# Gated unit and rotary queries finished in PSUM, rotary cache keys laid out by their loads, attention operands laid anew: one hybrid decoder step

## Chip, cores and metric

The kernel runs on one core of a Trainium2 chip. The metric is the device time of one execution in microseconds (us); the median of three runs stands for the kernel. TensorE (PE) multiplies and transposes into PSUM, VectorE (DVE), ScalarE (ACT) and GpSimd (POOL) work element by element, SyncE (SP) issues most DMAs; ACT and POOL issue some. Each engine runs its own list of instructions in a fixed order and waits on semaphores.

## What is computed

One step of a layer with two branches (an S5 state space and latent attention, MLA) for a prompt of 1024 tokens and for 8 sequences of 8 new tokens with 32 cache pages of 128 tokens each; width 1024, 16 heads, float32. Cut to what matters:

```python
xn = rmsnorm(x, norm_in)
u_s, g_s, cq, ckv_raw, kr_raw, g_a, m_s, m_a = split_in(xn @ w_in)
# S5 branch, then its gated unit
y = S5(u_s);  zg = gelu(y)
y_s = zg * sigmoid(zg @ ssm_w_glu + ssm_b_glu)
y_s = (y_s * silu(g_s)) @ w_br_ssm
# latent attention with rotary parts
cq = rmsnorm(cq, mla_q_norm);  q = einsum('blr,rhd->blhd', cq, mla_w_uq)
q_rope = apply_rope(q[..., QK_NOPE:], cos, sin)
ckv = rmsnorm(ckv_raw, mla_kv_norm);  k_rope = apply_rope(kr_raw, cos, sin)
o = attend(...)   # prompt: causal; new tokens: cached pages (cache_ckv, cache_krope by page_table) and themselves
y_a = (o * silu(g_a)) @ w_br_attn
h = x + (sigmoid(m_s) * y_s + sigmoid(m_a) * y_a) @ w_out;  y = rmsnorm(h, norm_final)
```

Besides `y` the step returns `ckv`, `k_rope` and the last S5 state, for the prompt and for the new tokens.

## The kernel before

A float32 product is made of three passes on float32r operands: each operand is split into a high and a low part (`split`, L96 the cast on ACT, L102 the subtraction on DVE or POOL), and `mm3` (L159) adds high by high, high by low and low by high in one PSUM bank. A weight stripe of 128 columns comes as `wraw`, is split into `whi` and `wlo`, and meets the transposed input `xT` in three chunks of 368, 368 and 352 tokens, 24 matmuls each. There are two PSUM banks of the name `mm` and six more of `tr`, `sc` and `acc`.

The stages are Python generators. `woven` interleaves two of them by weights, a scheduler turns the program into one order per engine, and `pin` holds a PE instruction to its place in the order in which it was written. In the order of time:

- up to 345 us: norm and transposes of x (`stage_x`), the S5 branch, gate stripes; `s5_states` (L780, L785) copies the last states to `sto`, one buffer, and SP writes them to `ssm_sample` and `ssm_prompt`;
- 345 to 480: two gate stripes, then `stage_latents`. `load_wide` (L137) loads the weights of the latents in pieces of 128 columns, `wraw` to `wwhi` and `wwlo`. The page numbers of the cache (`cache_rows`, `sel`, `j16`, `pt`, L1209 to L1219) are computed just ahead. `cqn` is the normed latent (L853, L868; its norm is a power on POOL, L200), transposed on PE at L835. Alongside runs `cache_ropes`: POOL gathers rotary keys of a page block into `dkr` (L1229, two buffers), copies them to `dks` in another order (L1234), PE transposes them (L1239), ACT and DVE split them, and SP writes three parts to `kr_dram` (L1244);
- 480 to 520: `q_rope`, rotary queries in 12 groups. DVE multiplies by the cosine table into `qr` (L904), POOL multiplies the rotated copy `qrot` by the sine table (L903), DVE adds (L905), then ACT and DVE split into `qh` and `ql`. One gate stripe is woven in, a second one is pinned behind;
- 520 to 700: latent queries, keys and values, gate stripes, then `attn_setup` (keys, queries, the `causal` mask at L983) and `dec_setup`, which also makes the rotary keys of the new tokens (`kss`, L1131 to L1136);
- 700 to 1130: the prompt attention (`prompt`: 32 units of head and half), woven with dense stages: gate stripes, the gelu of S5, then from 945 the gated unit `stage_glu`. A list of goals (`PLAN`) says at which mark of the attention each dense group is due;
- 1130 to 1545: `decode` over the 32 page blocks, woven with the end of the gated unit and with both branch products. POOL gathers `ck` (two buffers, L1201); ACT casts it to `ch`, POOL subtracts to `cl`, two halves of 1024 columns per page block (L102); `dec_keys` loads `krT` (L1251);
- to 1758: branch product of the attention and the output.

A gate stripe ends with a pass of ACT (L803) and one of DVE (`gst<-gst,mm`, L804), which empties the `mm` bank. In the gated unit a group ends with L1432 to L1440: ACT writes tanh of the bank to `th`, POOL adds `zz = zh + zl` (L1436), DVE computes `gl = (th + 1) * gl` (L1438) and `zz = zz * gl` (L1439), and SP writes `a_dram`. `gl` holds the gate, loaded from `g_gs` in four buffers.

## Time and profile before

| quantity | value |
|---|---|
| median of 3 runs | 1761.27 us (1760.45 to 1765.47) |
| the profiled execution | 1759.65 us |
| its span, first to last instruction | 1757.8 us |
| mean granted clock of PE | 0.987 |
| PE busy | 1688.1 us, 96% |
| DVE, ACT, POOL busy | 1158.4 (66%), 934.4 (53%), 592.5 us (34%) |
| DMA | 299.52 MB, 258309 packets, mean 170 GB/s |

Busy time counts an engine's instructions without overlap. A granted clock of 1.0 is 2.4 GHz on PE; 0.5 is 1.2 GHz, and a mean between the two is a mix of stretches at either level. In a timeline row the first number is the start in us of the span, the second the duration, and the bracket the idle time of the engine just before, with what ended it.

### The profile page before, as it was taken

How to read it: one execution, taken by the hardware profiler on the slowest of the kernel's cores; microseconds unless marked ns; L12 is line 12 of the kernel's file. 1: busy time of each engine (PE TensorE's matmuls, PEld its weight loads, DVE VectorE, ACT ScalarE, POOL GpSimd, SP SyncE). 2: the span in 40 equal slices, each digit the busy share in tenths (PEclk: the TensorE clock that was granted, in tenths of full speed). 3: DMA queues.
4: the chain of work that ended last, by engine and by line, in shares of the span. 5: the costliest groups of instructions: out<-in, count | busy, mean ns of one | idle time of the engine just before them, and what ended most of it. 6: DMA issues, size and time to landing. Idle time of an engine off the chain costs nothing.

```text
span 1757.8 us, 31271 instructions
## 1 busy us (share of the span) xinstructions
PE 1688.1 (96%) x10954; PEld 1588.1 (90%) x10954; DVE 1158.4 (66%) x2640; ACT 934.4 (53%) x2226; POOL 592.5 (34%) x622
## 2 busy tenths in 40 slices
PE   6999999989999999999998999999999999999997
PEld 5999999989989998999997898998988999899976
DVE  6768898333374343878888788567656666654496
ACT  5146657722354443767777556456656566631144
POOL 1000000013442204656663555654545445400012
PEclk9999999999999999999999999999999999999999
DMA  8555344544478988665667552575555455384322
GB/s 218 123 144 153 110 120 122 144 139 113 138 222 292 315 299 242 159 167 149 189 162 220 141 158 64 179 251 187 179 172 175 156 170 188 120 303 145 101 85 102
DMA packets 258309, 299.52 MB, mean 170 GB/s; under 512 B 40448, under 2 KB 215272, under 8 KB 251880
## 3 DMA queue, kind: packets, MB, share of 16 engines
q1 hardware_dynamic: 247976, 240.90, 47.7%
q0 software_dynamic: 7872, 48.24, 8.1%
q10 hardware_dynamic: 2304, 8.39, 1.3%
q8 instruction: 87, 1.43, 0.4%
q14 instruction: 70, 0.57, 0.1%
HBM read 201.79 MB, written 95.66 MB: 169 GB/s over the span
## 4 chain that ended last, share of the span: by engine, by line
PE 78%; DMA 8%; DVE 4%; issue 4%; ACT 3%; POOL 2%; SPq 1%; POOLq 0%; ACTq 0%; DVEq 0%
PE mm L159 40%; PE sc L1028 5%; PE sc L159 5%; PE acc L1193 4%; PE tr L1064 3%; PE tr L159 3%; DMA ck<-cache_ckv,pidx 2%; PE acc L1077 2%; PE acc L1078 2%; PE sc L1167 2%; PE sc L1256 1%; PE tr L1256 1%; PE tr L1167 1%; POOL cl L102 1%; DMA wraw<-w_in 1%
## 5 line engine op out<-in xcount | busy, mean ns | idle before, releaser
L159 PE MATMUL mm<-xT,whi 128*128 128x368 f32 (+1 forms) x1920 | 503.9, 336 | 8.7 <-ACT xT L253 4.8
L159 PEld LDWEIGHTS mm<-xT,whi 128*128 128x128 f32 x1920 | 340.9, 190 | 12.6 <-ACT xT L253 5.3
L159 PE MATMUL mm<-xT,wlo 128*128 128x368 f32 (+1 forms) x960 | 320.6, 334 | 0.2 <-DVE wlo L102 0.2
L102 POOL TENSOR_TENSOR cl<-ck,ch 128x1024 fp32r<-128x1024 f32 x64 | 154.2, 2411 | 163.8 <-ACT ch L96 149.4
L159 PEld LDWEIGHTS mm<-xT,wlo 128*128 128x128 f32 x960 | 182.4, 190 | 1.6 <-DVE wlo L102 0.5
L96 ACT CAST pTh<-tr 128x256 fp32r<-128x256 f32 (+1 forms) x248 | 110.8, 449 | 85.9 <-PE tr L1064 67.1
L102 DVE TENSOR_TENSOR pTl<-tr,pTh 128x256 fp32r<-128x256 f32 (+1 forms) x248 | 126.3, 512 | 41.2 <-ACT pTh L96 24.2
L1028 PE MATMUL sc<-K,Q 128*128 128x384 f32 (+5 forms) x576 | 131.5, 345 | 4.0 <-ACT p L1040 4.0
L1045 POOL TENSOR_SCALAR p<-p,sm 128x128 f32<-128x128 f32 (+7 forms) x128 | 96.8, 761 | 109.4 <-DVE sm L1044 48.5
L1040 ACT ACTIVATE p<-sc,sm 128x128 f32<-128x128 f32 (+2 forms) x192 | 110.7, 584 | 22.9 <-DVE sm L1035 12.7
L96 ACT CAST whi<-wraw 128x1024 fp32r<-128x1024 f32 (+1 forms) x76 | 73.3, 966 | 93.1 <-PE mm L159 79.9
L1229 POOL DMA_INDIRECT dkr<-cache_krope,pidx x32 | 33.0, 1032 | 264.2 <-DMA gkv<-mla_kv_norm 256.7
L1064 PE MATMUL tr<-ident,p 128*128 128x128 f32 x576 | 112.1, 274 | 7.6 <-DVE pTl L102 6.7
L159 PE MATMUL mm<-z,whi 128*128 128x368 f32 (+1 forms) x384 | 110.4, 349 | 2.3 <-ACT gst L801 2.3
L1032 DVE TENSOR_REDUCE sm<-sc 128x1 f32<-128x128 f32 (+2 forms) x192 | 104.2, 551 | 9.9 <-PE sc L1028 6.8
L159 PE MATMUL mm<-aT,whi 128*128 128x368 f32 (+1 forms) x384 | 107.6, 337 | 1.6 <-ACT th L1432 1.6
L1028 PEld LDWEIGHTS sc<-K,Q 128*128 128x128 f32 x576 | 98.3, 189 | 11.2 <-ACT p L1040 6.3
L159 PE MATMUL mm<-oT,whi 128*128 128x368 f32 (+1 forms) x384 | 94.2, 327 | 0.2 <-DVE gl L1464 0.2
L102 DVE TENSOR_TENSOR wlo<-wraw,whi 128x1024 fp32r<-128x1024 f32 (+1 forms) x54 | 61.6, 1142 | 39.7 <-ACT whi L96 36.1
L1064 PEld LDWEIGHTS tr<-ident,p 128*128 128x128 f32 x576 | 72.2, 140 | 14.3 <-DVE pTl L102 5.1
L96 ACT CAST ch<-ck 128x1024 fp32r<-128x1024 f32 x64 | 67.3, 1053 | 29.1 <-DMA ck<-cache_ckv,pidx 12.7
L1078 PE MATMUL acc<-pTl,Vt 128*128 128x256 f32 (+1 forms) x224 | 81.6, 364 | 0.1
(534 smaller groups left out, 4390.0 us busy)
## 6 DMA issues: line engine op xcount, KB each, us to landing
wraw<-w_in SPq DMA_DIRECT2D x45, 512.0 KB
krT<-kr_dram SPq DMA_DIRECT2D x64, 192.0 KB
kr_dram<-krx SPq DMA_DIRECT2D x64, 128.0 KB
...
```

What stands on the lines that cost most here:

```text
L96: nc.scalar.copy(hi, src)
L102: return e.tensor_sub(lo, src, hi.bitcast(F32))
L159: i = nc.tensor.matmul(ps, row(s, k)[:, wsl], row(m, k)[(slice(None),) + xsl], start=start and k == j == 0, stop=stop and k == nk - 1 and ...
L1028: self.mark(nc.tensor.matmul(s[:, :w], qq[:, i * P:(i + 1) * P], kk[:, k0:k0 + w], start=j == 0, stop=j == 2), j == 0)
L1032: V.reduce_max(sm[:, x:x + 1], s[:, :w], axis=AX.X)
L1040: nc.scalar.activation(p[:, k0:k0 + w], s[:, :w], AF.Exp, bias=sm[:, 2:3], scale=SCALE, accum_out=sm[:, 3 + x:4 + x])
L1045: nc.gpsimd.tensor_scalar(p[:, :n], p[:, :n], sm[:, 5:6], 0.0, op0=ALU.mult, op1=ALU.add)
L1064: self.mark(nc.tensor.transpose(b[:, x * P:(x + 1) * P], ptl[x][:, k * P:(k + 1) * P], self.ident), x == s0)
L1077: self.mark(nc.tensor.matmul(po[:, o0:], w, th[:, o0:], start=k == 0, stop=False))
L1078: nc.tensor.matmul(po[:, o0:], w, tl[:, o0:], start=False, stop=k == nk - 1)
L1167: i = nc.tensor.matmul(s, x[:, k], y[:, k], start=x is qlh and k == 0, stop=False)
L1193: self.mark(nc.tensor.matmul(o[:, :KV], t[:kp, i * P:(i + 1) * P], pv(i)[x], start=j == 0 and i == 0, stop=j == 2 and i == nt - 1), i == 0)
```

## The change

Eight edits in one kernel; line numbers behind L102 shift by 1 to 21.

1. `load_wide` issues its loads with a priority 400 earlier, the state writes of `s5_states` go to ACT's DMA queue, and `cache_rows` moves to the front of the program.
2. `cache_ropes` drops the copy `dks`: PE transposes the gathered tile as it came, the low part has a tile of its own (`krl`), and each part is written once. `dec_keys` then picks its rows by three loads with 512-byte pieces in place of one.
3. `q_rope` keeps the product and the sum in the PSUM bank, and all 12 groups are woven with two gate stripes.
4. `own_keys`, the rotary keys of the new tokens, leaves `dec_setup` and stands ahead of `q_rope`.
5. `attn_setup` allocates its operands in another order and splits all keys of one head before the next; `PLAN` moves its third group from marks 74 to 86 to marks 71 to 84.
6. The gated unit writes tanh back into the bank and finishes there: DVE multiplies (bank + 1) by `zr`, a row of z loaded from `z_dram`, then the bank by the gate, into the gate's own buffer, from which `a_dram` is written. POOL's additions are gone.
7. In `decode`, `cl` is computed in four pieces of 256 columns.
8. `osq` shares a buffer with `oms`, and a 320-byte tile `gap` is allocated.

```diff
-PLAN = ((6, MQ, MP - 1), (6, MP - 1, MP - 1), (3, MP + 2, MP + 14), (37, MP + 14, MD - 20), ...
+PLAN = ((6, MQ, MP - 1), (6, MP - 1, MP - 1), (3, MP - 1, MP + 12), (37, MP + 14, MD - 20), ...
...
-            nc.sync.dma_start(raw, self.a["w_in"][:, c0 + s:c0 + s + n].rearrange("(k p) c -> p k c", p=P))
+            with self.tc.high_priority(offset=UW):
+                nc.sync.dma_start(raw, self.a["w_in"][:, c0 + s:c0 + s + n].rearrange("(k p) c -> p k c", p=P))
...
-            nc.sync.dma_start(dst, st[:n])
+            nc.scalar.dma_start(dst, st[:n])
...
-            q = sb.tile([P, 368], F32, name="qr", bufs=2)[:, :m]
-            r = sb.tile([P, 368], F32, name="qrot", bufs=2)[:, :m]
+            r = sb.tile([P, 368], F32, name="qrot", bufs=4)[:, :m]
...
-            nc.vector.tensor_mul(q, b[:, :m], tabs[0][:, t0:t0 + m])
+            q = b[:, :m]
+            nc.vector.tensor_mul(q, q, tabs[0][:, t0:t0 + m])
             nc.vector.tensor_add(q, q, r)
...
+        for n in ("Q11", "K00", "K01", "causal", "Q00", "Q01", "K10", "K11", "Q10"):
+            t[n] = kp.tile([P, P], F32, name=n) if n == "causal" else kp.tile([P, SEQ], F32R, name=n)
...
-        kst = sb.tile([NS, P + NR], F32, name="kss", tag="p3", bufs=1)
+    def own_keys(self, lp, sb, ps):
+        kst = sb.tile([NS, P + NR], F32, name="kss", bufs=1)
...
-                ks = kss[j - 1] = sb.tile([P, 2, P], F32, name="dks", bufs=2)
-                nc.gpsimd.tensor_copy(ks.rearrange("p g (r i) -> p g r i", i=4), krs.pop(j - 1).rearrange("p g i r -> p g r i"))
...
-                for y, x in enumerate((hi, hi, lo)):
-                    nc.sync.dma_start(self.kr_dram[j - 2, :, y].rearrange("g p k -> p g k"), x.bitcast(F32))
+                for y, x in enumerate((hi, lo)):
+                    nc.sync.dma_start(self.kr_dram[j - 1, y], x.rearrange("p g k -> p (g k)").bitcast(F32))
...
-                self.split(*c, rows(b * 8 + g), "act", "pool")
+                src = rows(b * 8 + g)
+                nc.scalar.copy(c[0], src)
+                for i in range(4):
+                    Gp.tensor_sub(c[1][:, i], src[:, i], c[0][:, i].bitcast(F32))
...
-            nc.gpsimd.tensor_add(zz[:, :m].rearrange("p (c t) -> p c t", t=8), zh.rearrange("p t c -> p c t"),
-                                 zl.rearrange("p t c -> p c t"))
-            nc.vector.scalar_tensor_tensor(g[:, :m], th[:, :m], 1.0, g[:, :m], op0=ALU.add, op1=ALU.mult)
-            nc.vector.tensor_mul(zz[:, :m], zz[:, :m], g[:, :m])
-            nc.sync.dma_start(self.a_dram[rows, sl], zz[:, :m])
+            nc.scalar.activation(b, b, AF.Tanh, scale=0.25, bias=bg[:, j:j + 1])
+            nc.vector.scalar_tensor_tensor(b, b, 1.0, zr[:, :, t0 // 8:(t0 + m) // 8], op0=ALU.add, op1=ALU.mult)
+            g = g[:, :m].rearrange("p (c t) -> p c t", t=8)
+            nc.vector.tensor_mul(g, b.rearrange("p t c -> p c t"), g)
+            nc.sync.dma_start(self.a_dram[rows, sl].rearrange("r (c t) -> r c t", t=8), g)
...
+                zrow[j] = sb.tile([P, 8, NCK], F32, name="zr", bufs=1)
+                nc.sync.dma_start(zrow[j], self.z_dram[j * P:(j + 1) * P])
...
-                        yield from self.woven((ropes(), 17), (self.stage_gates(first=6, n=7, **gate), W5))
-                        yield from self.stage_gates(first=7, n=8, pin=True, **gate)
+                        self.own_keys(lp, sb, ps)
+                        yield from self.woven((ropes(), 17), (self.stage_gates(first=6, n=8, **gate), 2 * W5))
```

What this moves in the engines' lists, at three places; the numbers behind a name are those of its buffer. First SP ahead of the latents (345 to 375 us of the trace of before): the loads of `load_wide` are the `wraw` of L137, now L139. Before:

```order
L747 DMA y_dram_69<-Y_3841 16x8x136 x8
L785 DMA ssm_sample<-sto_3874 128x256
L785 DMA ssm_sample<-sto_3880 128x256
L785 DMA ssm_prompt<-sto_3886 32x256
L1209 DMA sel_4082<-k_sel 8x128
L1211 DMA j16_4084<-k_j16 128x1
L1213 DMA pt_4086<-page_table 8x32x1
L823 DMA gq_4113<-mla_q_norm 128x384
L824 DMA gkv_4114<-mla_kv_norm 128x256
L826 DMA rt_4117<-k_rope_tok 128x288
L137 DMA wraw_4121<-w_in 128x8x128
```

The same place on SP after the change:

```order
L750 DMA y_dram_69<-Y_3857 16x8x136 x8
L139 DMA wraw_4122<-w_in 128x8x128
L139 DMA wraw_4126<-w_in 128x8x128
L826 DMA gq_4113<-mla_q_norm 128x384
L827 DMA gkv_4114<-mla_kv_norm 128x256
L831 DMA rt_4117<-k_rope_tok 128x288
```

Nine rows stood between the last `y_dram` write and the first load, and none does now; the state writes and the page numbers are gone from this place.

Second, ACT at the same place, where `gst<-mm` is the first pass on a gate bank. Before:

```order
L803 ACTIVATE gst_3925<-mm_3928 128x368
L96 CAST whi_4529<-wraw_4527 128x1024
L803 ACTIVATE gst_3925<-mm_3955 128x352
L803 ACTIVATE gst_4014<-mm_3989 128x368
L96 CAST wwhi_4119<-wraw_4121 128x8x128
L96 CAST wwhi_4119<-wraw_4125 128x8x128
```

And ACT after the change:

```order
L788 DMA ssm_sample<-sto_3890 128x256
L788 DMA ssm_sample<-sto_3896 128x256
L806 ACTIVATE gst_3941<-mm_3916 128x368
L788 DMA ssm_prompt<-sto_3902 32x256
L806 ACTIVATE gst_3941<-mm_3944 128x368
L97 CAST wwhi_4120<-wraw_4122 128x8x128
L97 CAST wwhi_4120<-wraw_4126 128x8x128
L97 CAST whi_4529<-wraw_4527 128x1024
L806 ACTIVATE gst_3941<-mm_3971 128x352
```

The state writes stand between the gate passes, and the first two `wwhi` casts have moved ahead of the `whi` cast and of the gate pass of 352 columns.

Third, POOL in the decode, where `ck` is the gather of a page block (its buffer is that of the second block before it) and `cl` the low part of half a block. Before:

```order
L1201 DMA ck_16233<-cache_ckv,pidx_4092 128x2048
L102 TENSOR_TENSOR cl2_16312<-ck_16126,ch2_16311 128x1024
L102 TENSOR_TENSOR cl0_16372<-ck_16126,ch0_16371 128x1024
L1201 DMA ck_16375<-cache_ckv,pidx_4092 128x2048
L102 TENSOR_TENSOR cl1_16434<-ck_16233,ch1_16433 128x1024
L102 TENSOR_TENSOR cl2_16494<-ck_16233,ch2_16493 128x1024
```

After the change:

```order
L1215 DMA ck_16384<-cache_ckv,pidx_704 128x2048
L1333 TENSOR_TENSOR cl1_16445<-ck_16232,ch1_16444 128x256 x4
L1333 TENSOR_TENSOR cl2_16510<-ck_16232,ch2_16509 128x256 x4
L1215 DMA ck_16516<-cache_ckv,pidx_704 128x2048
L1333 TENSOR_TENSOR cl0_16606<-ck_16384,ch0_16605 128x256 x4
L1333 TENSOR_TENSOR cl1_16680<-ck_16384,ch1_16679 128x256 x4
```

Each subtraction is four in a row now; a gather still stands behind the subtractions of the block whose buffer it refills.

## Rows read from the trace of the kernel before

**Rows 1.** The page, part 1: busy us, share of the span, instructions.
```profile
PE 1688.1 (96%) x10954; PEld 1588.1 (90%) x10954; DVE 1158.4 (66%) x2640; ACT 934.4 (53%) x2226; POOL 592.5 (34%) x622
```
**Rows 2.** Stretches: length; busy PE, PEld, DVE, ACT, POOL (instructions); clock, DMA share, GB/s.
```profile
369.00:430.00 61.00, 56.57 (x336) 55.00 (x336) 19.61 (x41) 16.70 (x42) 16.28 (x23) 0.97 0.37 100
430.00:480.00 50.00, 46.51 (x324) 45.73 (x323) 16.42 (x43) 14.23 (x53) 25.31 (x59) 0.97 0.51 151
480.00:520.00 40.00, 35.71 (x214) 35.04 (x212) 33.51 (x53) 22.94 (x51) 21.69 (x22) 0.96 0.74 206
...
660.00:690.00 30.00, 26.38 (x157) 25.78 (x156) 8.69 (x24) 8.08 (x17) 12.37 (x19) 0.96 1.00 261
...
1000.00:1060.00 60.00, 58.94 (x376) 55.16 (x374) 50.76 (x141) 36.96 (x100) 31.49 (x31) 1.00 0.49 131
1060.00:1130.00 70.00, 66.48 (x410) 61.81 (x409) 48.93 (x112) 34.26 (x87) 38.55 (x33) 1.00 0.35 100
```
**Rows 3.** PE's waits by what ended them: us in total, times, longest.
```profile
PE tr L1256 <- DMA ck<-cache_ckv,pidx: 5.7, 4, 2.8
...
PE mm L159 <- DVE gst L804: 3.9, 2, 3.5
PE mm L159 <- ACT wwhi L96: 3.6, 1, 3.6
PE tr L835 <- DVE cqn L868: 3.5, 2, 2.0
...
PE tr L1136 <- DVE kss L1134: 1.8, 1, 1.8
```
**Rows 4.** Timeline ahead of the latents, SP, DVE, ACT and PE.
```profile
344.58 4.57 SPq L747 DMA_DIRECT2D y_dram<-Y  x8
349.24 3.02 SPq L785 DMA_DIRECT2D ssm_sample<-sto  x2
...
359.38 1.05 SPq L137 DMA_DIRECT2D wraw<-w_in  x2
...
351.45 0.43 DVE L780 COPY sto<-sc 128x256 f32<-128x256 f32 x1 [1.95 <-DMA ssm_sample<-sto]
...
364.37 1.05 ACT L96 CAST wwhi<-wraw 128x1024 fp32r<-128x1024 f32 x1 [3.57 <-DMA wraw<-w_in]
366.04 1.05 ACT L96 CAST wwhi<-wraw 128x1024 fp32r<-128x1024 f32 x1 [0.62 <-DMA wraw<-w_in]
...
360.96 0.61 PE L159 MATMUL mm<-xT,whi 128*128 128x368 f32 x2 [0.34 <-DVE gst L804]
```
**Rows 5.** Timeline in the latents, POOL: the copy `dks`.
```profile
445.99 0.61 POOL L1234 COPY dks<-dkr 128x256 f32<-128x256 f32 x1 [2.80 <-DMA kr_dram<-dks]
```
**Rows 6.** Timeline in the rotary queries, DVE and PE.
```profile
493.84 3.25 DVE L102 TENSOR_TENSOR ql<-qr,qh 128x352 fp32r<-128x352 f32 x1
...
517.99 0.98 PE L159 MATMUL mm<-xT,whi 128*128 128x368 f32 x2 [3.55 <-DVE gst L804]
```
**Rows 7.** DVE's waits from 660 to 690: us in total, times, longest.
```profile
DVE sc L1031 <- DMA causal<-k_causal: 4.4, 1, 4.4
```
**Rows 8.** Two DVE lines (ns least/median/most), and POOL and DVE in the gated unit.
```profile
L804 DVE SCALAR_TENSOR_TENSOR gst<-gst,mm x48: 502/529/540, 267.4 to 709.4; 128x368 f32<-128x368 f32 x32, 128x352 f32<-128x352 f32 x16
...
L1438 DVE SCALAR_TENSOR_TENSOR gl<-th,gl x24: 513/543/2498, 984.4 to 1189.3; 128x368 f32<-128x368 f32 x16, 128x352 f32<-128x352 f32 x8
...
1026.71 2.39 POOL L102 TENSOR_TENSOR wlo<-wraw,whi 128x1024 fp32r<-128x1024 f32 x1
...
1026.98 2.50 DVE L1438 SCALAR_TENSOR_TENSOR gl<-th,gl 128x352 f32<-128x352 f32 x1
```
**Rows 9.** POOL lines (ns least/median/most; busy us, mean ns), and the cache gathers.
```profile
L102 POOL TENSOR_TENSOR cl<-ck,ch x64: 2360/2394/3027, 1134.4 to 1530.4; 128x1024 fp32r<-128x1024 f32 x64
...
DMA to landing us min/median/max: 5.6/6.1/10.2
...
L1408 POOL TENSOR_TENSOR gw<-gw,gy 128x156 f32<-128x156 f32 x48 | 25.1, 523 | 2.7
```

More of the change, by code (lines that the diff above doesn't have):

```diff
@@ L193, in constants @@
         self.qr_dram = d.tile([2, 2, H * 16, TOK], F32, name="qr_dram")
-        self.kr_dram = d.tile([DB * 4, 2, 3, P, P], F32, name="kr_dram")
+        self.kr_dram = d.tile([DB * 4, 2, P, 2 * P], F32, name="kr_dram")
     def rnorm(self, out, ss, n, scr):
@@ L825, in stage_latents @@
         rt = sb.tile([P, 9, 2, NR // 2], F32, name="rt", bufs=1)
+        sb.tile([P, 80], F32, name="gap", bufs=1)
         nc.sync.dma_start(rt, a["k_rope_tok"])
@@ L995, in attn_setup @@
                 nc.tensor.transpose(b[:, i * P:(i + 1) * P], kst[:, i], self.ident)
[L996 to L998 removed]
+            banks.append(b)
+        for h, rows in ((0, slice(64, 128)), (1, slice(0, 64))):
+            hi, lo = self.KTs[h]
+            for half, b in enumerate(banks):
+                c = slice(half * 512, half * 512 + 512)
                 self.split(hi[rows, c], lo[rows, c], b[rows], "act", "dve")
@@ L1223, in cache_ropes @@
         nc, a = self.nc, self.a
-        krs, kss = {}, {}
+        krs = {}
         n = DB * 4
-        for j in range(n + 2):
+        for j in range(n + 1):
             if j < n:
```

58 lines of the change are left out of this document (30 added, 28 removed).

## Prediction

> **What bounds the kernel now.** The page comes first: TensorE (PE) is busy 1688.1 us of a span of 1757.8 [rows 1]. The change leaves every matmul and transpose in place, so no engine's total is the bound to look at: what can be won is PE's idle time, 1757.8 − 1688.1 = 69.7 us, and the time that PE runs at the lower of its two clock levels. The second view is PE's busy time by stretch. The length of a stretch less PE's busy time is its idle time, and its length times (1 − granted clock) is what the 1.2 GHz level costs in place of 2.4. Six stretches in which the change works are idle for 61 − 56.57 = 4.4, 50 − 46.51 = 3.5, 40 − 35.71 = 4.3, 30 − 26.38 = 3.6, 60 − 58.94 = 1.1 and 70 − 66.48 = 3.5 us, 20.4 together [rows 2]. Third come PE's waits by cause, which name what ends last in them: `wwhi`, `gst`, `cqn` and `kss` [rows 3]. Last, the timelines of these places tell what the late producer was itself waiting for [rows 4 to 9]. Idle time of VectorE (DVE), ScalarE (ACT) and GpSimd (POOL) is left aside except where PE waits behind it.
>
> **The change part by part.**
>
> *Latent weights loaded earlier.* PE waits 3.6 us for `wwhi` [rows 3] and the stretch is idle 4.4; its granted clock of 0.97 costs 61 × 0.03 = 1.8 [rows 2]. The cause is SP's queue: the `y_dram` writes end at 349.15, then two `ssm_sample` writes, of which the first starts at 349.24 though its data were ready, and the first `wraw` loads start only at 359.38 [rows 4]. Now ACT issues the state writes and the loads stand straight behind `y_dram`. They still need the place of the state tile, so they wait for three writes after each other at 2.2 us each (349.24 to the copy at 351.45 [rows 4]). Started at about 344.6 on ACT, and held by DVE's gate pass at 349.0, the third lands near 352, and the loads leave then, 7 us earlier. The third load follows 7 us earlier as well: the stall of 4.4 and its clock loss of 1.8 should go. A new wait comes in. On ACT two `wwhi` casts now stand ahead of the next `whi` cast and of the `gst` pass that empties a gate bank. By the landings of before (359.38 to 364.37 and to 366.04, 5.0 and 6.7 us [rows 4]) the two casts start at 357 and 358.7, `whi` ends at 360.7, the pass at 361.2, and on DVE `wwlo`, `wlo` and the second pass follow until about 362.6. PE wants that bank at 360.3, where it already waits until 360.96 [rows 4]: about 2 us more. Behind that pass stand the next gate passes; PE waits for them. Sum −4.4 − 1.8 + 2.0 = **−4.2**; −6.2 if the loads land early, −2 if this wait too brings the low clock level.
>
> *Rotary keys of the cache.* The POOL copy `dks` goes, with its wait for `kr_dram`. At 445.99 this copy started after 2.80 us of waiting [rows 5] and held the norm behind it, for which `cqn` and then PE were late: `cqn` cost PE 3.5 us in two waits, the longer 2.0 [rows 3]. The shorter, 1.5, belongs to the copy; the longer is the last chain of the stage, which stays. PE's transposes now wait for the gather itself, with two buffers; a gather starts when the transposes two pages earlier are done, at least 71 matmuls and transposes before its own; at 35.71 / 214 = 0.17 us each [rows 2] that is 12 us, more than the longest flight of the larger cache gathers, 10.2 [rows 9]. Sum **−1.5** (0 to −3.5). Writes to `kr_dram` fall from three per page block to two; the later reads rise from one instruction to three, 128 more on SP. SP is not a bound there, so I take nothing.
>
> *Rotary queries in PSUM, woven with two gate stripes.* A DVE instruction with two SBUF inputs took 3.25 us at 493.84 [rows 6], where a gate pass of the same width takes 0.53 [rows 8]; I read it as waiting for POOL, as in the pair of [rows 8]. PE then waits 3.9 us for `gst` in two waits, 3.55 of it at 517.99 [rows 3, 6], behind gate passes that stand in DVE's queue after such instructions. The stretch is idle 4.3 and loses 40 × 0.04 = 1.6 to the clock [rows 2]. After the change each of these instructions reads one operand from PSUM; the gate pass, which does so already, took 502 to 540 ns in all 48 cases, whatever POOL did [rows 8]. The bank is held longer, for which the second stripe gives cover (72 more matmuls, 12 us at 0.17). Sum −4.3 − 1.6 + 0.9 left over = **−5.0** (0 to −5.9).
>
> *Own keys moved, attention operands laid anew, third group of the plan earlier.* The stretch is idle 3.6 us and loses 1.2 to the clock, with the DMA engines at a share of 1.00 [rows 2]; 1.8 is the wait for `kss` [rows 3], which sits on DVE behind an instruction that waits 4.4 us for the load of `causal` [rows 7]. Taking `kss` out of that queue ends this wait, but `causal` still lies behind large loads, so the first softmax can be what is late next; some 13 more gate matmuls (at 26.38 / 157 = 0.17 us [rows 2], 2.2 us) stand ahead of the second one. I take half of 4.8: **−2.4** (0 to −4.8).
>
> *Gated unit finished in PSUM.* POOL loses 24 additions. On DVE the line that they feed took 543 ns in the median and 2498 at worst [rows 8]: at 1026.98 it starts just behind a POOL `wlo` that runs from 1026.71 to 1029.10, and ends at 1029.48, just behind it. The two stretches are idle 4.6 us [rows 2], mostly just behind such instructions. Against this stand 8 loads of 544 KB with a single buffer, which DVE meets early enough except in the dense last stripes (1 to 2 us, inside the slack of two gate banks), and SP, which must wait for an `a_dram` write before it can reload `gl` (24 times, some 2 us by the 2.2 of [rows 4]); what is queued behind it on SP are attention loads issued a unit ahead. Sum −4.6 + 0.6 = **−4.0** (+3 to −5).
> The Trainium skill ("SBUF — State Buffer", "SBUF: two separate sides") states that DVE with two SBUF inputs and a POOL instruction reading SBUF exclude one another for a whole instruction; these rows agree, and by it the sum stands. Against the change speaks "VectorE: DVE Perf Modes" ("Rules for kernel authors"), which advises copying a matmul's output to SBUF if many operations follow on it; by that the chains would be slower in PSUM and these two terms would shrink to nothing, a total of −6.5; the 529 ns median of the gate pass beside 543 [rows 8] shows no such price.
>
> *Cache values in four pieces on POOL.* 64 subtractions of 1024 columns at 2360 ns or more become 256 of 256. POOL took 523 ns for 156 columns [rows 9]: (2360 − 523) / 868 = 2.12 ns a column and 193 ns fixed, so a piece takes 735 ns and four take 2.94 us, 0.58 more per half page, 37 us of POOL in all. POOL has room, but the gather of the next page stands behind the second half, lands 5.6 to 10.2 us later [rows 9], and PE already waits for 4 of them, 5.7 us [rows 3]. Delays of 0.6 to 1.2 us reach PE where the slack is under that. In return DVE meets holds of 0.74 in place of 2.4. Sum **+1.6** (−2 to +8).
>
> Total: −4.2 − 1.5 − 5.0 − 2.4 − 4.0 + 1.6 = −15.5 us. The profiled execution took 1759.65 (span 1757.8 and 1.85 around it), so 1744.2; the median of the runs, 1761.27, lies 1.6 above it, so 1745.8. I say **1745**.
>
> **The rivals.**
>
> *The stalls move on.* PE runs its order as written. If the wait at 360 lasts 3 us and brings the low level (−4.2 becomes −1), `causal` is late next (0), the longer `cqn` wait grows by what is won before it (−0.5), and rope banks are 2 us late (−3): −1 − 0.5 − 3 − 0 − 4 + 1.6 = −7, **1754**. For it: the DMA share of 1.00 [rows 2] and ACT's new order. Against it: the largest terms are tied to instructions that go.
>
> *Queues held by the new waits.* The `gl` reloads hold SP for 24 × 2.2 = 53 us. If a quarter of that reaches PE through late K, Q and value loads, 13 us of the gain are lost: **1757 to 1762**, no change. Against it: no PE wait for these loads is among the causes now.
>
> *Slower: the gathers.* If the decode is a ring (gather, transposes, cast, four pieces, next gather) without slack, each of 32 pages adds 2 × 0.58 = 1.2 us, 37 us, less the 14 to 17 won elsewhere: about 1780. It decides from the point where the slack is under 1.2 in more than 14 pages; with 20 pages late, 24 us: **1768**. For it: four PE waits already, up to 10.2 us of flight [rows 3, 9]. Against it: 28 pages show none.
>
> *DVE is slow for another reason.* If its long instructions are not tied to POOL, moving operands to PSUM gains nothing: −4.2 − 1.5 − 2.4 + 1.6 = −6.5, **1755**. The gate pass's narrow 502 to 540 ns [rows 8] speaks against it.
>
> **How the numbers follow.** Forecast (1735 to 1753) 0.58; stalls moved, or DVE slow for another reason (1753 to 1757) 0.18; queues held (1757 to 1764) 0.10; gathers (above 1766) 0.09; better than 1735, where every term takes its lower bound (−23), 0.05. A measurement of this kernel can tell about 0.3%, 5.3 us, from no change. Faster than 1756: 0.58 + 0.05 + 0.14 = 0.77; within: 0.04 + 0.10 = 0.14; slower than 1766.6: 0.09. The range leaves out the slow case and the ends: 1732 to 1761.
>
> **What would show it.** Right: no wait of PE for `wwhi` near 369, none for `gst` near 515, one `cqn` wait left, DVE's gated-unit instructions all near 530 ns, POOL less busy up to 1180 and some 37 us busier behind it, PE at 97% of its span. Wrong: a PE wait for `gst` near 360 over 3 us; more than 6 us of waits for `ck`; K or Q loads among PE's causes; clock losses that stay where the stalls go.

## The result, and the profile after

| | before | after |
|---|---|---|
| median of 6 runs | 1763.26 us (1759.83 to 1766.29) | 1745.13 us (1737.97 to 1749.05) |
| ratio, 95% interval | | 0.9895 (0.9871 to 0.9919) |
| profiled execution, its span | 1759.65, 1757.8 us | 1745.78, 1743.9 us |
| mean granted clock | 0.987 | 0.991 |

The forecast was 1745 with a range of 1732 to 1761; the time is 1745.1. The sum came out; most of its terms did not, as the rest of this text shows, so that the agreement to 0.1 us is luck.

The page of the changed kernel, part 1 (against [rows 1]), and its costliest POOL group (busy us, mean ns, idle time before it):

```profile
PE 1684.2 (97%) x10954; PEld 1586.0 (91%) x10954; DVE 1140.2 (65%) x2640; ACT 933.0 (53%) x2226; POOL 567.4 (33%) x758
```

```profile
L1333 POOL TENSOR_TENSOR cl<-ck,ch 128x256 fp32r<-128x256 f32 x256 | 189.8, 773 | 149.4 <-ACT ch L1331 148.7
```

PE's idle time fell from 69.7 to 1743.9 − 1684.2 = 59.7 us. The same stretches as in [rows 2], with the columns given there:

```profile
345.00:369.00 24.00, 18.20 (x100) 17.90 (x99) 7.61 (x10) 5.78 (x8) 0.98 (x1) 0.90 0.75 216
369.00:430.00 61.00, 61.00 (x366) 59.77 (x366) 19.40 (x41) 15.58 (x42) 11.98 (x16) 0.98 0.28 84
430.00:480.00 50.00, 47.44 (x341) 46.64 (x340) 19.12 (x51) 16.29 (x56) 20.11 (x53) 1.00 0.46 138
480.00:520.00 40.00, 40.00 (x249) 39.84 (x248) 25.55 (x52) 22.59 (x51) 17.01 (x17) 1.00 0.80 245
...
1000.00:1060.00 60.00, 59.96 (x388) 57.16 (x386) 48.72 (x147) 37.42 (x101) 25.16 (x26) 1.00 0.57 158
1060.00:1130.00 70.00, 69.09 (x430) 65.83 (x429) 41.28 (x106) 34.87 (x84) 29.33 (x30) 1.00 0.57 174
```

PE has no idle time left in 369 to 430 and in 480 to 520, and 0.04 and 0.91 us in the two stretches of the gated unit. A new hole of 5.8 us has opened just ahead, between 345 and 369; before, that stretch was idle 0.3 us:

```profile
345.00:369.00 24.00, 23.66 (x143) 23.12 (x141) 7.08 (x12) 5.32 (x8) 2.74 (x3) 1.00 0.69 199
```

PE's waits by cause say what the hole is (against [rows 3]):

```profile
PE mm L161 <- DVE gst L807: 7.0, 2, 5.8
PE tr L1075 <- DVE pTl L103: 4.7, 7, 1.8
PE tr L1270 <- DMA ck<-cache_ckv,pidx: 4.2, 4, 1.4
PE sc L840 <- DVE cqn L873: 2.6, 1, 2.6
...
PE sc L1270 <- DMA ck<-cache_ckv,pidx: 1.1, 1, 1.1
```

`wwhi` and `kss` are gone, one `cqn` wait is left, and the largest wait for `gst` (5.8 in place of 3.5) is at another place.

Both programs have 10,954 matmuls and transposes, so the start of the k-th one in either trace tells about how far the change is ahead at that point of the work (about, since the change also reorders some of them). Start in the change minus start before, in us, worked out from the two traces; a minus says that the change is ahead:

| time in the kernel after | 310 | 400 | 446 | 493 | 541 | 685 | 736 | 927 | 1029 | 1124 | 1176 | 1357 | 1495 | end |
|---|---|---|---|---|---|---|---|---|---|---|---|---|---|---|
| after minus before | −0.7 | +0.4 | +0.7 | −1.8 | −9.9 | −12.2 | −9.6 | −7.1 | −12.3 | −19.8 | −16.5 | −20.6 | −14.6 | −13.1 |

The gain is made mostly in two places: the rotary queries with the end of the latents (10.6 us between 446 and 541) and the stretch of the gated unit (12.7 between 927 and 1124); 2.3 come between 541 and 685. It is given back mostly in two: the attention up to 927 (5.1 from 685 on) and the decode (5.2 between 1124 and 1495).

### The profile page after: what moved, and what is told of

It reads as the page before. It is cut to its first block, busy times and chain, and to the rows that moved or that the text cites. A ratio compares the mean times of both kernels' runs of the same rounds, so it can differ in the third digit from the quotient of the medians.

```text
span 1743.9 us, 31564 instructions
## 1 busy us (share of the span) xinstructions
PE 1684.2 (97%) x10954; PEld 1586.0 (91%) x10954; DVE 1140.2 (65%) x2640; ACT 933.0 (53%) x2226; POOL 567.4 (33%) x758
## 4 chain that ended last, share of the span: by engine, by line
PE 78%; DMA 9%; DVE 5%; ACT 4%; issue 2%; POOL 2%; SPq 1%; POOLq 0%; ACTq 0%; DVEq 0%
PE mm L161 41%; PE sc L161 5%; PE sc L1039 5%; PE acc L1207 4%; PE tr L1075 3%; PE tr L161 3%; DMA ck<-cache_ckv,pidx 3%; PE acc L1089 2%; PE acc L1088 2%; PE sc L1270 2%; PE sc L1181 1%; PE tr L1270 1%; PE tr L1181 1%; DMA wraw<-w_in 1%; POOL cl L1333 1%
## 5 line engine op out<-in xcount | busy, mean ns | idle before, releaser
L1333 POOL TENSOR_TENSOR cl<-ck,ch 128x256 fp32r<-128x256 f32 x256 | 189.8, 773 | 149.4 <-ACT ch L1331 148.7
L103 DVE TENSOR_TENSOR pTl<-tr,pTh 128x256 fp32r<-128x256 f32 (+1 forms) x248 | 126.6, 512 | 34.7 <-ACT pTh L97 26.0
L1051 ACT ACTIVATE p<-sc,sm 128x128 f32<-128x128 f32 (+2 forms) x192 | 110.9, 583 | 31.1 <-DVE sm L1048 14.8
L103 DVE TENSOR_TENSOR wlo<-wraw,whi 128x1024 fp32r<-128x1024 f32 (+1 forms) x54 | 61.4, 1136 | 44.5 <-ACT whi L97 44.3
L1075 PEld LDWEIGHTS tr<-ident,p 128*128 128x128 f32 x576 | 71.9, 141 | 12.6 <-DVE pTl L103 6.3
```

The lines of the kernel that those rows point to most:

```text
L103: return e.tensor_sub(lo, src, hi.bitcast(F32))
L1051: nc.scalar.activation(p[:, k0:k0 + w], s[:, :w], AF.Exp, bias=sm[:, 2:3], scale=SCALE, accum_out=sm[:, 3 + x:4 + x])
L1075: self.mark(nc.tensor.transpose(b[:, x * P:(x + 1) * P], ptl[x][:, k * P:(k + 1) * P], self.ident), x == s0)
L1333: Gp.tensor_sub(c[1][:, i], src[:, i], c[0][:, i].bitcast(F32))
```

## The experiments

Every run is the changed kernel with one part undone or mended, next to the kernel before in the same set. The kernel before gave medians of 1757.69 to 1763.26 in four sets, so a difference to 1745.13 carries some 3 us of doubt from the set alone. The table therefore gives both comparisons, and I take as shown only what both say, or what a stretch of the trace shows by itself. No run undoes by itself the move of the page numbers, the second gate stripe or edit 8.

| run | median, us | ratio to before (95%) | to the change: by medians, by difference of ratios x 1763 |
|---|---|---|---|
| casts_behind | 1744.66 | 0.9915 (0.9885 to 0.9945) | −0.5, +3.5 |
| loads_as_before | 1746.29 | 0.9932 (0.9912 to 0.9951) | +1.2, +6.5 |
| key_copy_as_before | 1750.42 | 0.9930 (0.9904 to 0.9956) | +5.3, +6.2 |
| ropes_in_sbuf | 1750.63 | 0.9942 (0.9921 to 0.9963) | +5.5, +8.3 |
| attention_as_before | 1738.07 | 0.9899 (0.9861 to 0.9936) | −7.1, +0.7 |
| plan_as_before | 1741.85 | 0.9896 (0.9862 to 0.9929) | −3.3, +0.2 |
| own_keys_as_before | 1734.73 | 0.9850 (0.9821 to 0.9879) | −10.4, −7.9 |
| glu_as_before | 1751.84 | 0.9947 (0.9926 to 0.9968) | +6.7, +9.2 |
| unit_in_sbuf_no_add | 1749.09 | 0.9952 (0.9929 to 0.9976) | +4.0, +10.0 |
| cl_in_one | 1736.03 | 0.9860 (0.9825 to 0.9896) | −9.1, −6.2 |
| cl_one_casts_behind | 1733.16 | 0.9866 (0.9838 to 0.9894) | −12.0, −5.1 |
| three_repairs | 1730.31 | 0.9833 (0.9806 to 0.9860) | −14.8, −10.9 |

Only four of these intervals lie outside that of the change (0.9871 to 0.9919): ropes_in_sbuf, glu_as_before and unit_in_sbuf_no_add above it, three_repairs below. Six of the twelve times fell where the theory on record put them (of these, ropes_in_sbuf and loads_as_before without the waits that it named); plan_as_before and key_copy_as_before missed by under 1 us, and casts_behind, cl_in_one, attention_as_before and own_keys_as_before missed by more.

All these programs have the same number of matmuls too. The time that the same matmuls take, in us, one trace for each run, shows how much a stretch varies when its code is left alone:

| stretch, by its time in the change | before | change | runs that leave its code as in the change | runs that undo a part of it |
|---|---|---|---|---|
| 446 to 541 | 105.5 | 95.0 | 94.7 to 97.9 | key_copy_as_before 102.3, ropes_in_sbuf 96.6 |
| 685 to 927 | 236.9 | 242.0 | 241.8 to 242.5, once 245.4 | own_keys_as_before 240.6, plan_as_before 239.7, attention_as_before 237.2, three_repairs 238.0 |
| 927 to 1124 | 209.7 | 196.9 | 197.0 to 201.5 | glu_as_before 210.9, unit_in_sbuf_no_add 204.4 |
| 1176 to 1495 | 317.1 | 319.0 | 310.5 to 321.8 | cl_in_one 310.4, cl_one_casts_behind 310.8, three_repairs 309.3 |

In the decode one trace of the same code differs from another by up to 11 us, so a few us there in a single trace show nothing.

### Latent weights: where the new wait comes from

The timeline of the changed kernel at this place (start, duration, row; SP, ACT, DVE, PE; against [rows 4]):

```profile
343.64 6.19 ACTq L788 DMA_DIRECT2D ssm_sample<-sto  x2
...
343.87 6.01 SPq L750 DMA_DIRECT2D y_dram<-Y  x8
...
348.99 0.43 DVE L783 COPY sto<-tr 128x256 f32<-128x256 f32 x1 [5.38 <-DMA ssm_sample<-sto]
...
354.17 1.02 SPq L139 DMA_DIRECT2D wraw<-w_in  x2
...
359.74 1.04 ACT L97 CAST wwhi<-wraw 128x1024 fp32r<-128x1024 f32 x1 [6.49 <-DMA wraw<-w_in]
361.32 1.04 ACT L97 CAST wwhi<-wraw 128x1024 fp32r<-128x1024 f32 x1 [0.54 <-DMA wraw<-w_in]
362.27 1.04 ACT L97 CAST whi<-wraw 128x1024 fp32r<-128x1024 f32 x1
363.22 0.46 ACT L806 ACTIVATE gst<-mm 128x352 f32<-128x352 f32 x1
...
364.68 0.52 DVE L807 SCALAR_TENSOR_TENSOR gst<-gst,mm 128x352 f32<-128x352 f32 x1
...
365.25 0.98 PE L161 MATMUL mm<-xT,whi 128*128 128x368 f32 x2 [5.80 <-DVE gst L807]
```

The first state write on ACT now runs beside the eight `y_dram` writes and lands 348.99 − 343.64 = 5.4 us after its issue, where it took 2.2 behind them. The loads leave at 354.17, the casts begin at 359.74, and the gate pass of 352 columns stands behind three casts on ACT and three subtractions on DVE.

**casts_behind**: the casts and subtractions of the latents' first three pieces are ordered behind the gate passes.

```diff
-            self.split(hi[:, :, s:s + n], lo[:, :, s:s + n], raw, "act", "dve")
+            i = nc.scalar.copy(hi[:, :, s:s + n], raw)
+            v = nc.vector.tensor_sub(lo[:, :, s:s + n], raw, hi[:, :, s:s + n].bitcast(F32))
+            if c0 == C_CQ:
+                for x, y in zip((i, v), passes[s // P]):
+                    self.behind(x, y)
```

> The changed kernel, with the three wwhi casts of the latents (and their wwlo subtractions) held behind the gate passes that empty the mm banks; the loads themselves stay early. Theory (the order on ACT and DVE makes the wait): PE's wait of 5.8 us for gst near 359 us falls under 1 us, the granted clock of 345 to 430 us returns from 0.90 and 0.98 to 1.00, and no wait for wwhi comes back near 369; the time falls by 6 to 9 us to 1736 to 1739. Rival (the loads still land too late, after 359.7 us): the wait only moves to the latents' first matmul, 3 to 5 us for wwhi or wwlo, and the time stays within 3 us of 1745.

The wait of 5.8 is gone; in 345 to 369 PE is busy 22.48 us at clock 1.00. In its place stand two short waits for the third piece. Its load leaves at 361.50 (362.07 in the change), but its cast starts 5.9 us later, at 367.37, where it started 3.9 us later in the change:

```profile
368.47 0.44 PE L166 MATMUL mm<-wwhi,xT 128*128 128x384 f32 x1 [1.43 <-ACT wwhi L141]
...
369.73 0.44 PE L166 MATMUL mm<-wwlo,xT 128*128 128x384 f32 x1 [0.82 <-DVE wwlo L142]
```

By matmul number it gains 3.9 us on the change up to 417 and gives 2.9 back by 477, where the clock is 0.93 in 430 to 480. So the order of the casts causes the wait, but the time as a whole is the same as that of the change within its doubt. The loss of clock need not come: in cl_one_casts_behind and three_repairs, which have the same edit, the matmuls from 310 to 541 take 224.5 and 224.8 us, against 231.1 in the change and 230.1 here.

**loads_as_before**: the early priority and ACT's state writes undone; the page numbers stay in front.

```diff
-            with self.tc.high_priority(offset=UW):
+            if True:
...
-            nc.scalar.dma_start(dst, st[:n])
+            nc.sync.dma_start(dst, st[:n])
```

> The changed kernel with the latents' weight loads at their old priority and the state writes back on SP; the page numbers stay in front; PE's order is the same. Theory (the early loads trade one stall for another): the wait of 5.8 us near 359 us goes, one for wwhi of 3 to 5 us near 368 comes back, and the time is within 3 us of 1745. Rival (the early loads pay, as forecast): 1748 to 1751.

The loads leave at 355.53, 8.9 us after the last `y_dram` write; that was 10.2 before [rows 4] and is 4.3 in the change. PE still waits for the gate pass (3.97 us at 365.49) behind two casts, and no wait for `wwhi` comes back. The same stretches as above:

```profile
345.00:369.00 24.00, 20.03 (x114) 19.73 (x113) 6.84 (x11) 6.25 (x9) 0.00 (x0) 0.93 0.71 204
369.00:430.00 61.00, 61.00 (x380) 59.53 (x379) 22.65 (x46) 17.18 (x46) 13.14 (x18) 1.00 0.29 81
430.00:480.00 50.00, 47.43 (x324) 46.84 (x324) 18.14 (x49) 15.34 (x53) 20.10 (x53) 0.97 0.48 146
```

PE is busy 128.5 us of the 135, against 126.6 in the change and 23.66 + 56.57 + 46.51 = 126.7 before. The early loads gain nothing here. The runs are 1 to 6 us slower than the change by the two measures; in the trace the loss comes only behind 927 (7.3 us up to the end), in code that is the same in both.

### Rotary keys and rotary queries

**key_copy_as_before**: the copy `dks`, three writes per block and the single `krT` load again.

```diff
+                ks = kss[j - 1] = sb.tile([P, 2, P], F32, name="dks", bufs=2)
+                nc.gpsimd.tensor_copy(ks.rearrange("p g (r i) -> p g r i", i=4), krs.pop(j - 1).rearrange("p g i r -> p g r i"))
...
-                for y, x in enumerate((hi, lo)):
-                    nc.sync.dma_start(self.kr_dram[j - 1, y], x.rearrange("p g k -> p (g k)").bitcast(F32))
+                for y, x in enumerate((hi, hi, lo)):
+                    nc.sync.dma_start(self.kr_dram[j - 2, :, y].rearrange("g p k -> p g k"), x.bitcast(F32))
```

> The changed kernel with the rotary cache keys copied on POOL again (dks), three writes to kr_dram per page block and one load per krT. Theory (the copy costs one cqn wait of 1.5 us and its clock, and holds DVE beside the rotary queries): the cqn waits are two again, the stretch from 430 to 520 us is 2 to 4 us longer, 1747 to 1750. Rival (the shorter loads of 512 bytes and 128 more DMAs on SP cost as much in the decode): 1742 to 1746 with fewer waits for ck.

The second `cqn` wait is back (two, 3.9 us), and so is idle time in the rotary queries, although these still work in PSUM. PE by stretch, then POOL, DVE and PE at one place:

```profile
430.00:480.00 50.00, 46.09 (x319) 44.99 (x318) 17.17 (x49) 14.80 (x53) 23.83 (x58) 0.97 0.52 150
480.00:520.00 40.00, 37.49 (x229) 36.80 (x228) 25.35 (x52) 22.29 (x51) 19.97 (x22) 1.00 0.76 223
```

```profile
510.99 0.65 POOL L1248 COPY dks<-dkr 128x256 f32<-128x256 f32 x1 [5.75 <-DMA kr_dram<-dks]
511.61 0.94 POOL L907 TENSOR_TENSOR qrot<-qrot,tab 128x352 f32<-128x352 f32 x1
...
512.58 0.53 DVE L910 TENSOR_TENSOR tr<-tr,qrot 128x352 f32<-128x352 f32 x1 [3.52 <-POOL qrot L907]
...
514.58 0.41 PE L1253 MATMUL tr<-ident,dks 128*128 128x128 f32 x2 [1.44 <-DVE ql L103]
```

The copy waits for a DMA write, the product `qrot` is queued behind it on POOL, DVE behind `qrot`, PE behind DVE. Undoing this edit alone costs 7.4 us between 445 and 546, two thirds of what the change gains there: 3.1 by 480, in the latents, and 4.3 behind 510, in the queries.

This doesn't say that the copy made PE wait there in the kernel before. There the only copy between 480 and 520 that waited for a DMA waited 1.28 us, and DVE worked without a longer pause than 0.2 us from 492.8 until the gate pass that PE awaits at 517.99 [rows 6]:

```profile
509.68 0.65 POOL L1234 COPY dks<-dkr 128x256 f32<-128x256 f32 x1 [1.28 <-DMA kr_dram<-dks]
512.82 1.91 DVE L905 TENSOR_TENSOR qr<-qr,qrot 128x368 f32<-128x368 f32 x1
517.43 0.51 DVE L804 SCALAR_TENSOR_TENSOR gst<-gst,mm 128x352 f32<-128x352 f32 x1
```

So before, DVE's long instructions stood ahead of PE; with these gone and the copy kept, the copy's wait stands there instead.

**ropes_in_sbuf**: product and sum in SBUF again, the weaving of all groups with two stripes kept.

```diff
-            r = sb.tile([P, 368], F32, name="qrot", bufs=4)[:, :m]
+            q = sb.tile([P, 368], F32, name="qr", bufs=2)[:, :m]
+            r = sb.tile([P, 368], F32, name="qrot", bufs=2)[:, :m]
...
-            q = b[:, :m]
-            nc.vector.tensor_mul(q, q, tabs[0][:, t0:t0 + m])
+            nc.vector.tensor_mul(q, b[:, :m], tabs[0][:, t0:t0 + m])
```

> The changed kernel with the rotary queries' product and sum back in SBUF (qr, two buffers, qrot two buffers); the weaving with two gate stripes stays. Theory (PSUM operands end DVE's holds): DVE again has cases of 1 to 3 us from 480 to 520 us, and PE waits 2 to 5 us there, time up 3 to 6 us with the clock. Rival (the second gate stripe's cover did it): DVE's holds return but PE's idle time in that stretch stays under 1 us, and the time is within 2 us of 1745.

```profile
480.00:520.00 40.00, 40.00 (x248) 39.84 (x248) 26.59 (x49) 22.13 (x49) 18.43 (x17) 1.00 0.79 239
520.00:545.00 25.00, 23.84 (x155) 22.44 (x154) 11.31 (x22) 10.78 (x28) 4.38 (x3) 1.00 0.85 287
```

In 480 to 520 PE is never idle here either; the stage loses 1.6 us in all, which is inside what the stretch varies when its code is left alone. DVE's instructions with two SBUF inputs are still held at times, but the worst takes 1282 ns for the sum and 843 for `ql`, where before they took up to 1905 and 3254. The rest of the 5 to 8 us appears in the trace only behind 927, in the gated unit and the decode (7.0 us of waits for `ck` against 5.3), far from the edit, by no more than these stretches vary by themselves; its path isn't settled.

### Attention

**own_keys_as_before**: `own_keys` back in `dec_setup` and the old allocation and split order, the new `PLAN` kept. **plan_as_before**: the old third group, the rest kept. **attention_as_before**: both.

```diff
-        for n in ("Q11", "K00", "K01", "causal", "Q00", "Q01", "K10", "K11", "Q10"):
+        self.causal = kp.tile([P, P], F32, name="causal")
...
-                        self.own_keys(lp, sb, ps)
...
-PLAN = ((6, MQ, MP - 1), (6, MP - 1, MP - 1), (3, MP - 1, MP + 12), ...
+PLAN = ((6, MQ, MP - 1), (6, MP - 1, MP - 1), (3, MP + 2, MP + 14), ...
```

> The changed kernel with the own keys back in dec_setup, the attention's operands allocated and split as before, and the third group of PLAN at its old marks. Theory (this part gains about 1.3 us near 680 us and loses about 4 in the attention up to 930 us, so it is worth nothing): PE waits again for kss or the first softmax near 680 us, 2 to 4 us, and the total is within 3 us of 1745. Rival (the part gains 2.4 us as forecast): 1747 to 1750. Rival (the attention's loss of 4 us belongs to it): 1740 to 1743.

> The changed kernel with own keys and attention operands as before; PLAN stays as changed. Theory (PLAN carries the loss, and moving the own keys gains its wait of 1.8 us): 1745 to 1748, PE waits for kss again 1 to 2 us. Rival (the operands' order carries the loss): 1738 to 1741.

> The changed kernel with only the third group of PLAN back at its old marks; own keys and operands stay as changed. Theory (the earlier gate group takes cover away from the later attention units, so PLAN carries the loss of the attention): 1738 to 1741, PE's idle time from 700 to 945 us falls by 3 to 5 us. Rival (the loss lies with the operands' order): within 3 us of 1745.

Two stretches of the four kernels: the change, own keys and operands as before, `PLAN` as before, both as before.

```profile
640.00:740.00 100.00, 95.22 (x586) 89.44 (x584) 60.94 (x166) 53.84 (x153) 48.86 (x72) 1.00 0.77 211
740.00:860.00 120.00, 116.58 (x748) 109.69 (x747) 98.66 (x297) 85.84 (x263) 74.01 (x110) 1.00 0.62 169
```

```profile
640.00:740.00 100.00, 97.80 (x604) 91.98 (x603) 62.05 (x180) 55.02 (x157) 51.05 (x75) 1.00 0.76 210
740.00:860.00 120.00, 116.25 (x748) 109.46 (x747) 97.90 (x296) 86.69 (x264) 72.75 (x107) 1.00 0.63 170
```

```profile
640.00:740.00 100.00, 96.55 (x593) 90.73 (x592) 59.93 (x177) 56.01 (x160) 51.69 (x78) 1.00 0.75 206
740.00:860.00 120.00, 118.22 (x759) 110.96 (x758) 96.20 (x295) 88.06 (x264) 73.25 (x108) 1.00 0.65 175
```

```profile
640.00:740.00 100.00, 96.99 (x591) 91.59 (x590) 58.68 (x180) 55.44 (x158) 50.95 (x76) 0.98 0.74 203
740.00:860.00 120.00, 118.41 (x761) 111.47 (x760) 95.85 (x296) 88.13 (x265) 73.41 (x108) 1.00 0.65 175
```

The two halves cost PE time in different stretches: the operand order 2.6 us in 640 to 740, the new plan 1.6 in 740 to 860. With the new order, a key split waits 3.99 us for ACT at 669.49, and `causal` still lands late (a wait of 3.67 at 673.85, in place of 4.4 [rows 7]); the gate pass queued behind makes PE wait 1.17 at 675.17. With the new plan, gelu instructions of DVE (`gy<-gw,gy`, 128x156, median 322 ns) take up to 2760 ns, against 1847 with the plan as before and 1178 with both halves as before; that PE's loss comes from these isn't shown. By matmul number the loss is plain: from 541 to 927 the change takes 386.1 us, and with own keys and operands, the plan or both as before 382.9, 383.6 and 382.4, so the part costs 3.7 us, and undoing either half wins most of it. By runs, own keys and operands as before gain 8 to 10 us, more than these stretches hold; the rest shows in the decode, where traces of the same code differ by more than that. Undoing both gains 7 by one measure and nothing by the other.

### Gated unit

**glu_as_before**: `th` and `zz` in SBUF and POOL's additions again, and no loads of `zr`.

```diff
-            nc.scalar.activation(b, b, AF.Tanh, scale=0.25, bias=bg[:, j:j + 1])
-            nc.vector.scalar_tensor_tensor(b, b, 1.0, zr[:, :, t0 // 8:(t0 + m) // 8], op0=ALU.add, op1=ALU.mult)
+            nc.gpsimd.tensor_add(zz[:, :m].rearrange("p (c t) -> p c t", t=8), zh.rearrange("p t c -> p c t"), ...
+            nc.vector.scalar_tensor_tensor(g[:, :m], th[:, :m], 1.0, g[:, :m], op0=ALU.add, op1=ALU.mult)
+            nc.vector.tensor_mul(zz[:, :m], zz[:, :m], g[:, :m])
```

> The changed kernel with the gated unit alone put back (tanh to SBUF, POOL adds zz, both DVE multiplications between two SBUF tiles). Theory (this part is worth most of the gain from 945 to 1210 us, where the changed kernel runs 12.7 us ahead and gives 3.7 back): the time rises by 6 to 11 us to 1751 to 1756, DVE's two lines of the unit again have single cases of 2 us and more. Rival (the gain there came from elsewhere, the relief of POOL by other parts or the new order of the attention): within 3 us of 1745.

**unit_in_sbuf_no_add**: only the tanh goes to an SBUF tile `th`; the loads of `zr` stay, POOL adds nothing.

```diff
-            nc.scalar.activation(b, b, AF.Tanh, scale=0.25, bias=bg[:, j:j + 1])
+            th = sb.tile([P, 368], F32, name="th", bufs=1)
+            th = th[:, :m].rearrange("p (t c) -> p t c", t=8)
+            nc.scalar.activation(th, b, AF.Tanh, scale=0.25, bias=bg[:, j:j + 1])
```

> The changed kernel with the gated unit's tanh written to an SBUF tile (one buffer), so that both DVE multiplications have two SBUF inputs again, but with z loaded and no addition on POOL. Theory (two SBUF inputs wait for whatever POOL runs): single cases of 1.5 us and more stay among the unit's DVE lines, and the time lies between the changed kernel and the one with the unit as before, 1747 to 1751. Rival (POOL's additions and their wait for a_dram were the whole cost): DVE lines near 540 ns at most 700, and the time within 2 us of 1745.

DVE's lines of the unit (ns least/median/most), in the change and then in unit_in_sbuf_no_add:

```profile
L1450 DVE SCALAR_TENSOR_TENSOR mm<-mm,zr x24: 517/540/550, 974.9 to 1171.0; 128x368 f32<-128x368 f32 x16, 128x352 f32<-128x352 f32 x8
...
L1452 DVE TENSOR_TENSOR gl<-mm,gl x24: 508/530/542, 976.0 to 1176.2; 128x368 f32<-128x368 f32 x16, 128x352 f32<-128x352 f32 x8
```

```profile
L1452 DVE SCALAR_TENSOR_TENSOR th<-th,zr x24: 510/554/2410, 969.9 to 1175.6; 128x368 f32<-128x368 f32 x16, 128x352 f32<-128x352 f32 x8
...
L1454 DVE TENSOR_TENSOR gl<-th,gl x24: 787/814/2207, 971.0 to 1179.0; 128x368 f32<-128x368 f32 x16, 128x352 f32<-128x352 f32 x8
```

With one input in PSUM all 48 take 508 to 550 ns; with both in SBUF the same work takes up to 2410, although POOL has no part in the unit any more. In glu_as_before the worst is 2934, PE's waits for `pTl` grow from 4.7 to 10.0 us, and it is 12.6 us behind the change at 1136, 7.7 at the end. The two runs can't be told apart by their ratios, but their traces differ: from 974, just ahead of the unit's first DVE instruction, to 1124, glu_as_before loses 12.5 us on the change and unit_in_sbuf_no_add 7.7. So the operand in PSUM counts for more than half of the loss here; the rest goes with the additions, but by one trace each, where the code alone varies by up to 4.6 us. The 814 ns median is a second cost: this line reads `th` with a stride, from SBUF here and at 530 ns from PSUM in the change.

The long cases go with POOL. In the kernel before, all 22 instructions of the rotary queries and the gated unit with two SBUF inputs that took over 700 ns end 0.37 to 0.41 us after the end of a POOL instruction; in unit_in_sbuf_no_add all eight over 1 us do so within 0.38 to 0.56.

### Decode

**cl_in_one**: `cl` in one piece of 1024 columns.

```diff
-                src = rows(b * 8 + g)
-                nc.scalar.copy(c[0], src)
-                for i in range(4):
-                    Gp.tensor_sub(c[1][:, i], src[:, i], c[0][:, i].bitcast(F32))
+                self.split(*c, rows(b * 8 + g), "act", "pool")
```

> The changed kernel with the cache values' subtraction in one instruction of 1024 columns. Theory (pieces cost 0.58 us per half page on POOL, and gathers leave later): POOL busy falls by 30 to 36 us, PE's waits for ck fall from 5.3 us to 2 to 4, the time falls by 1 to 3 us. Rival (short pieces pay, because DVE no longer stands 2.4 us behind POOL): PE's waits for DVE in the decode rise and the time rises by 2 to 5 us.

Two stretches of the decode, in the change and in cl_in_one, and POOL's line in the latter:

```profile
1300.00:1400.00 100.00, 97.69 (x660) 90.56 (x659) 65.45 (x138) 62.58 (x129) 56.03 (x77) 0.98 0.54 169
...
1400.00:1500.00 100.00, 96.95 (x662) 89.45 (x661) 65.80 (x136) 59.88 (x125) 55.87 (x76) 1.00 0.52 165
```

```profile
1300.00:1400.00 100.00, 99.27 (x678) 91.53 (x677) 69.74 (x142) 62.81 (x130) 50.04 (x29) 1.00 0.57 181
1400.00:1500.00 100.00, 99.37 (x684) 92.00 (x684) 67.87 (x141) 64.71 (x132) 50.50 (x28) 1.00 0.53 165
```

```profile
L103 POOL TENSOR_TENSOR cl<-ck,ch 128x1024 fp32r<-128x1024 f32 x64 | 153.4, 2399 | 176.8 <-ACT ch L97 176.6
```

POOL is busy 36 us less, PE's waits for `ck` fall from 5.3 to 1.1 us, and the two kernels, within 0.5 us of each other up to 1124, part by 10.2 us until 1539. Only 4.2 of it are waits for `ck`; the others are short waits for `cT`, products later in the same chain (4.9 us in the change, 0.6 here), and the clock. The decode varies by itself, but the other traces say the same: from 1176 to 1495 the nine with this decode in pieces take 316.5 us in the mean (310.5 to 321.8), the three with one instruction 310.2 (309.3 to 310.8).

### Mended versions

**cl_one_casts_behind** joins two of the edits above, **three_repairs** adds attention_as_before.

> The changed kernel with both repairs: the cache values' subtraction in one instruction and the wwhi casts held behind the gate passes. Theory (each repair keeps its own part: 9 us in the decode, 0 to 3 us before the latents): 1733 to 1737. Rival (the gain of the single subtraction was a lucky phase of the gathers, which another start of the latents upsets): above 1740.

> The changed kernel with three repairs: one subtraction, casts behind the gate passes, and the attention's setup and PLAN as before. Theory (the attention's part of the change costs 4 to 7 us by itself and adds to the others): 1726 to 1731. Rival (its loss shows only beside the slow gathers, which the single subtraction has already cured): within 3 us of 1733.

Neither adds up: casts_behind brings at most 3 us to cl_in_one by medians and nothing by ratio. three_repairs is the fastest of all, 1.67% below the kernel before (interval 1.40 to 1.94%) and, by the two measures, 11 to 15 us below the change.

## Why the prediction was right, and where it was not

The time was right by luck: errors of both signs cancelled. Term by term, with the stretch's own gain from the table of the k-th instruction:

- **Latent weights earlier: −4.2 forecast, about +1 measured** (−0.7 at 310, +0.4 at 400). The steps that failed are two. "The third lands near 352" took 2.2 us for each state write; the first took 5.4 beside the `y_dram` writes. And "about 2 us more" for the new wait followed from it: the second pass ended at 365.2 in place of 362.6, and PE lost 5.8 us and ran at a granted clock of 0.50 from 365 to 371. The text's own sign for wrong, a wait over 3 us near 360, came true. Its mechanism, casts ahead of the pass on ACT, is what casts_behind confirms. The `wwhi` wait did go, but it is gone in loads_as_before too.
- **Rotary keys −1.5 and rotary queries −5.0 forecast, −10.6 measured together.** The sum was too small, and its split can't be read from the runs, since the two edits cover for each other. For the kernel before, the reading of the stall at 517.99 holds: DVE's long instructions stood ahead of the gate pass. But key_copy_as_before shows what ending them wins while the copy stays, 3.2 us (102.3 against 105.5): the copy's wait for its DMA then reaches PE in the queries, through POOL's queue, and with the loss in the latents this costs 7.4 in place of the 1.5 that I gave the copy for one `cqn` wait. [rows 5] showed such a wait of 2.80 at 445.99, and I did not ask what it would hold up once DVE was faster. ropes_in_sbuf shows that with the copy gone and a second stripe as cover the PSUM operands are worth no more than 1.6 us in the stage. They do end the holds: all 24 instructions of the two lines take 517 to 550 ns.
- **Own keys, operands, plan: −2.4 forecast, a loss of 2 to 4 us measured** (in 640 to 860 PE is busy 211.8 us; 215.4 with both halves as before, of which the clock of 0.98 takes 2.0; by matmul number 3.7 from 541 to 927). The wait for `kss` went, as said. "The first softmax can be what is late next" was right in kind, but I credited half the gain anyway; `causal` came as late as before, and both halves of the edit cost PE time of their own. The bound of 0 excluded a loss without a reason from the rows; that was the fault.
- **Gated unit: −4.0 forecast, −12.7 in its stretch, 7 to 9 over the program** by glu_as_before. Of the 12.7, 2.4 come by 974, ahead of the unit's first DVE instruction, and some 2 may be chance: with the same unit the stretch takes 196.9 to 201.5 us. The mechanism was right to the number (instructions "all near 530 ns": 508 to 550). What was mis-sized is the idle time: I took that of two stretches, 4.6 us. For the matmuls from 974 to 1124 (983.5 to 1143.8 before) PE's idle time fell from 6.3 to 0.1 us, with 3.4 us of waits for the attention's `pTl` among it, since the holds made that late too; a fall of the clock also went (0.99 before from 1010.8 on, 1.00 after), some 1.3 us. The rest of these 10.3 us isn't settled.
- **Cache values in pieces: +1.6 forecast, 6 to 9 measured**, at or past the far end of its bound of +8. The costs on POOL were right (737 ns a piece against 735, 35.6 us more in all against 37). The step that failed is the slack: I counted only pages whose waits were already seen as late. Against the kernel before, only 5.2 us of loss show, since the decode with one instruction is by now 3 to 4 us shorter than before (from 1124 to 1495: 361.4 to 362.4 against 365.7 us); which edit did that, or whether it is more than chance, isn't settled.
- **The rivals.** "Stalls move on" is what happened at 360 and in the attention, but two larger gains outweighed it. The gathers' rival had the right mechanism, at a quarter of its price of 24 to 37 us. Queues held by the `gl` reloads did not show: no K, Q or value load is among PE's causes. "DVE slow for another reason" fell: the long cases go with operands in SBUF (unit_in_sbuf_no_add) and end with a POOL instruction; only its price, nothing won, is near what ropes_in_sbuf lost in the rotary queries.
- PE at 97%, POOL busier by 36 us in the decode, no `wwhi` wait near 369, no `gst` wait near 515 and one `cqn` wait came as written. One sum of the prediction is wrong: its lower bounds add up to −6.2 − 3.5 − 5.9 − 4.8 − 5.0 − 2.0 = −27.4, not −23; the class below 1735 goes with −27.4.

The Trainium skill ("SBUF — State Buffer", section "SBUF: two separate sides") states that a DVE instruction with two SBUF inputs and a POOL instruction that reads SBUF shut each other out for a whole instruction; the traces agree, with 508 to 550 ns against up to 2410. The Trainium skill ("VectorE: DVE Perf Modes", section "Rules for kernel authors") offers for work on a matmul's output either to accept the rate from PSUM or to copy it to SBUF first if many operations follow; here, with two operations to follow, the unit with its tanh in SBUF was 4 to 10 us slower (unit_in_sbuf_no_add).
